# Low products at the end of each weight unit, chunk outputs written by ScalarE's queue, shifted reads spaced, last norm on VectorE alone

## The chip, the core and the metric

The kernel runs on one core of one Trainium2 chip. The metric is the device time of one execution in microseconds (us); a change within 0.5% of it counts as no change. Six parts are changed together in this case, most of them in the first quarter of the program.

## What is computed

One layer of a hybrid decoder for 320 columns of tokens (256 of a prompt, and 8 samples of 8). A normalised input h goes through one combined projection into three mixers side by side, and a SwiGLU block follows:

```
h = rmsnorm(x);  proj = h @ w_in             # 2048 -> a_val, a_gate, b_u, b_v, c_u
A: z = a_val * sigmoid(a_gate); 31-tap causal depthwise conv of z; layer norm per head; silu
B: chunks of 128 positions: u * (tril(w_s) @ layernorm(v) + b_s)
C: per group of 16 channels a complex diagonal state of 64 (h_t = a h_{t-1} + B u_t),
   y = Re(C h) + d u;  z = gelu(y);  gl = z @ w_glu;  out = gl_1 * sigmoid(gl_2)
x += concat(A, B, C) @ w_out;   x += (silu(h2 @ w_gate) * (h2 @ w_up)) @ w_down
y = rmsnorm(x)                               # and the new states
```

## The kernel before

**Units.** The large weights come from DRAM in units of eight 128x128 tiles (512 KB, tile `raw`, SyncE's queue, L201). ScalarE rounds a unit to `hi` (L208), VectorE takes the rest, `lo = raw - hi` (L215, recorded at L52). TensorE makes three products of each tile: `hi` by the high part of the input (L237), `hi` by its low part (L238), `lo` by the high part (L240); 24 products for a unit. There are three buffers each of `raw` and `hi`, two of `lo`. Three accumulators in PSUM are called `acc`, two `sm`, three `sc`. Unit u's loop body (L1297 on) loads unit u + 3, splits `hi` of u + 2 and `lo` of u + 1, and then issues its products in four quarters.

**The order of units.** ORDER (L26) lists the projection: C tiles (inputs of the state mixer), K0 to K3 (the convolution of a head, 32 small products of 128x32 weights and more, L577), A and U tiles, and V (L1018 to L1022, the `v` rows in products of 512 columns). The loop over all other weights follows from about 320 us on.

**Side work.** Everything else (recurrence, preparation of states, norms, gates) is written as generators that yield. After each quarter of a unit `Side.run` (L122) steps those with priority under 1, and then VectorE's work (priority 1 and over) as long as VectorE's modelled time `vec.t` is not past TensorE's modelled time `pe`. So this rule alone sets where VectorE's recurrence operations stand among the `lo` splits, and through waits such as `until` also where TensorE's products of the mixers stand among the units.

**Convolution reads.** `conv_in` (L541 on) writes a head's row to DRAM (`zr`), and reads it back in four shifted copies `z4` by GpSimd's queue (L556); `row_load` brings the next head's row.

**State mixer's output.** A group of 128 channels i (0 to 7, called y0 to y7 here) is computed by products with the states H (L914 to L916). ScalarE applies the gelu and gives `z` (L922). `z_layout` (L927 on) writes z to DRAM (`dz`, SyncE's queue), waits, and reads it back in another layout as `zc` (four reads); the GLU products read zc (L949, L950).

**Tail.** After the last unit the norm's row `r` is made, and 16 tiles of the output are multiplied by it and written out (L1366 to L1370).

Of the kernel before, what the change touches and what calls it, by code (L numbers as in the profile page):

```python
# [15 lines left out]
NT = 320  # L16
# [4 lines left out]
MULT, ADD, SUB = ALU.mult, ALU.add, ALU.subtract  # L21
# [10 lines left out]
def build(nc, tc, I, O):  # L32
    with ExitStack() as ctx:
        ctx.enter_context(tc.manual_schedule())
        _build(ctx, nc, tc, I, O)
# [65 lines left out]
class Side:  # L101
# [22 lines left out]
    def run(self):  # L124

        self.now += 1
        for t in list(self.live):
            if t.prio < 1 and t.due <= self.now and not t.done:
                self.step(t)
        skip = None  # L130
        while self.vec.t <= self.pe:
            ready = [t for t in self.live if t.due <= self.now and t.prio >= 1]
            if not ready:
                break
            t = ready[0]
            if t is skip:
                if len(ready) > 1 and ready[1].prio < GAP:
                    t = ready[1]
                else:
                    self.vec.t += 0.13  # L140
            skip = t if self.step(t) == "gap" else None
        self.vec.t = max(self.vec.t, self.pe - 0.5)
# [12 lines left out]
def _build(ctx, nc, tc, I, O):  # L155
    A, G, T = nc.scalar, nc.gpsimd, nc.tensor
    V = Vec(nc.vector)
    side = Side(V)
# [11 lines left out]
    def acc():  # L170
        return pacc.tile([128, 512], F32, tag="acc", name="acc")
# [4 lines left out]
    def sc():  # L176
        return psc.tile([128, 512], F32, tag="sc", name="sc")
# [4 lines left out]
    def tmp(tag, shape=(128, NT), dt=F32, bufs=1):  # L182
        return mp.tile(list(shape), dt, tag=tag, name=tag, bufs=bufs)
# [4 lines left out]
    S = {}  # L188
# [28 lines left out]
    class Box:  # L217
        ps = None

    def tile_units(src, rows, post, need=None, psum=acc):  # L220

        n = src.shape[1] // 128
        box = Box()

        def make(u, m):
            def pre():
                if need is not None:
                    need()
                if u == 0:
                    box.ps = psum()  # L230

            def mm(hi, lo, a, b):
                r = rows()
                ps = box.ps[:, :NT]
                for j in range(a, b):
                    c = slice(j * 128, j * 128 + 128)
                    T.matmul(ps, hi[:, c], r[u + j][0], start=u + j == 0, stop=False)  # L237
                    T.matmul(ps, hi[:, c], r[u + j][1], start=False, stop=False)  # L238
                for j in range(a, b):
                    T.matmul(ps, lo[:, j * 128:j * 128 + 128], r[u + j][0], start=False, stop=u + j == n - 1)  # L240
            return pre, mm

        out = []
        for u in range(0, n, 8):
            m = min(8, n - u)
            pre, mm = make(u, m)
            out.append((src[:, u * 128:(u + m) * 128], m * 128, mm, m * 0.44, pre,
                        (lambda: post(box.ps[:, :NT])) if u + m == n else None))
        return out
# [71 lines left out]
    E = Later(V)  # L321
# [206 lines left out]
    def post_val(h):  # L528
        def f(ps):
            row, gs, r = S["row", h], S["gs", h], S["rstd"]  # L530
            V.scalar_tensor_tensor(gs, gs, 1.0, ps, op0=ADD, op1=MULT)
            V.scalar_tensor_tensor(row[:, 30:286], gs[:, 0:NP], 0.5, r[:, 0:NP], op0=MULT, op1=MULT)
            V.scalar_tensor_tensor(samples(row)[:, :, 30:38], gs[:, NP:].rearrange("p (s t) -> p s t", s=8), 0.5,
                                   r[:, NP:].rearrange("p (s t) -> p s t", s=8), op0=MULT, op1=MULT)
            side.add(0.3, conv_in(h))
        return f

    def row_load(h):

        S["row", h] = tmp("row", (128, ZW), bufs=2)  # L540
        G.dma_start(S["row", h], I["rows"][h])  # L541

    def conv_in(h):

        row = zrows[h]
        yield Wait(2)
        G.dma_start(row, S["row", h])
        yield Wait(5)
        if h < 2:
            row_load(h + 2)  # L550
        while h and ("k", h - 1) not in S:
            yield Wait(1)
        z4 = S["z4", h] = tmp("z4", (128, 4, Z4))
        base = row[0:1, 0:1]
        for g in range(4):
            G.dma_start(z4[:, g], bass.AP(tensor=base.tensor, offset=base.offset + 32 * g * ZW,  # L556
                                           ap=[[1, 4], [ZW, 32], [1, Z4]]))

    def k_pre(h):
        def f():  # L560
            side.until(lambda: ("z4", h) in S)
            S["kps", h] = acc()
        return f

    def k_mm(h):
# [337 lines left out]
    def c_out():  # L903

        H, U = S["H"], S["U"]
        side.add(0.3, c_glu())
        for i in range(8):
            while side.now < S.get(("mat due", i), 1e9) or i - S["glu"] >= 3 or ("rec", i // 4) not in S:
                yield Wait(1)
            bd, Tt = S["mats"].pop(i)  # L910
            py = sc()
            for p in range(4):
                o = py[:, 80 * p:80 * p + 80]
                T.matmul(o, cat(bd[:, 0, p, 1:5]), H[:, 0, 4 * i + p, 0:80], start=True, stop=False)  # L914
                T.matmul(o, cat(bd[:, 1, p, 1:5]), H[:, 1, 4 * i + p, 0:80], start=False, stop=False)  # L915
                T.matmul(o, Tt[:, p, :], U[:, i, p, :], start=False, stop=True)  # L916
            side.pe += 1.65
            S["y"] = i + 1
            z = tmp("z", (128, 4, 80))
            py = py[:, :NT].rearrange("p (a q) -> p a q", a=4)  # L920
            for c in (slice(0, 64), slice(64, 80)):
                A.activation(z[:, :, c].rearrange("p a (b r) -> p a r b", b=8),  # L922
                             py[:, :, c].rearrange("p a (r b) -> p a r b", b=8), AF.Gelu_apprx_tanh)
            side.add(0.2, z_layout(i, z))
            yield Wait(2)

    def z_layout(i, z):  # L927
        zc = S["zc", i] = tmp("zc", (128, 4, 80), bufs=3)
        dz = dp.tile([128, 4, 80], F32, tag="dz", name="dz")
        yield Wait(2)  # L930
        nc.sync.dma_start(dz, z)
        yield Wait(4)
        for p in range(4):
            nc.sync.dma_start(zc[32 * p:32 * p + 32], dz[:, p, :].rearrange("(j g) q -> g j q", j=4))
        S["z due", i] = side.now + 3

    def c_glu():
        crows, half = [], {}
# [232 lines left out]
    def rstd2(neg=False):  # L1171
        if "rstd" not in Q:
            g = inv_sqrt(Q["fp"], Q["pv"][:, :NT], [128, NT], "rs2", neg, 16.0)
            while "rstd" not in Q:
                try:
                    next(g)
                except StopIteration as e:
                    Q["rstd"] = e.value
        return Q["rstd"]
# [64 lines left out]
    for t in ORDER:  # L1244
        if t[0] == "A":
            a_tiles(int(t[1]))
        elif t[0] == "K":
            h = int(t[1])
# [48 lines left out]
    for u, d in enumerate(units):  # L1297
# [31 lines left out]
        if u in (100, 102, 104, 106):  # L1329
            h = (u - 100) // 2  # L1330
# [13 lines left out]
        n = d["n"] // 128  # L1344
# [16 lines left out]
    r = rstd2(True)  # L1361

    def rows(q, a, b):
        return X["xa"][q][:, a:b, :]

    for E, q, a, b in ((G, 3, 0, 2), (G, 3, 2, 4), (V, 0, 0, 1), (V, 0, 1, 4), (V, 1, 0, 4), (V, 2, 0, 3), (V, 2, 3, 4)):  # L1366
        E.tensor_tensor(rows(q, a, b), rows(q, a, b), r[:, None, :].to_broadcast([128, b - a, NT]), op=MULT)
    for E, q, a, b in ((nc.sync, 0, 0, 1), (nc.scalar, 0, 1, 4), (nc.sync, 3, 0, 2), (nc.scalar, 1, 0, 4),
                       (nc.sync, 3, 2, 4), (nc.scalar, 2, 0, 3), (nc.sync, 2, 3, 4)):
        E.dma_start(O["yT"][:, 4 * q + a:4 * q + b, :], rows(q, a, b))  # L1370

_OUT = {
    "yT": (128, 16, 320), "rows": (4, 128, ZW), "nss": (128, 2, 32, 9), "ncv": (64, 512),
# [86 lines left out]
```

## Time and profile before

| what | value |
|---|---|
| median of 3 runs | 1352.18 us (1348.64 to 1353.87) |
| the profiled execution | 1352.68 us, span 1351.0 us |
| mean granted TensorE clock | 0.989 of full speed |
| TensorE busy | 1318.4 us, 98% of the span |
| VectorE busy | 721.8 us, 53% |
| ScalarE busy | 565.8 us, 42% |

The span is the time from the first to the last recorded instruction; the time of the execution is 1.7 us longer. PE is TensorE, DVE is VectorE, ACT is ScalarE, POOL is GpSimd, SP is SyncE; a q behind a name is the engine's own instruction queue. The granted clock is a share of 2.4 GHz; 0.5 is the lower of its two levels, 1.2 GHz.

### The profile page before, as it was taken

The numbers are of one execution on the slowest core, as the hardware profiler recorded it, in microseconds if no ns is written. First come the engines' busy times: TensorE is split into PE (matmuls) and PEld (weight loads), VectorE is DVE, ScalarE is ACT, GpSimd is POOL, SyncE is SP. The second block draws the span as 40 slices with busy tenths as digits, with TensorE's granted clock in tenths as the row PEclk, the third lists the DMA queues.
The fourth block names the chain that finished last, engine by engine and source line by source line (L and its number), as shares of the span: only waits on it lengthen the run. The fifth ranks groups of instructions, "written<-read, shape, count | busy, mean of one in ns | idle before, by whom it ended". The sixth has DMA issues, their size and how long they took to land.

```text
span 1351.0 us, 22667 instructions
## 1 busy us (share of the span) xinstructions
PE 1318.4 (98%) x9324; PEld 1290.4 (96%) x9324; DVE 721.8 (53%) x1195; ACT 565.8 (42%) x824; POOL 71.9 (5%) x101
## 2 busy tenths in 40 slices
PE   8999999999999999999999999999999999999995
PEld 8888987899999999999999999999999999999995
DVE  8867986685555444444444444444444444434444
ACT  7378535474454333333333333333233333322452
POOL 1110101010130000000000000000000000000112
PEclk9999998999999999999999999999999999999998
DMA  7784576564444554444444444555444445554453
GB/s 261 194 204 133 142 187 161 168 210 141 149 147 142 175 173 148 148 141 157 155 146 151 141 157 155 147 150 152 146 156 145 152 141 158 155 148 141 142 152 121
DMA packets 78584, 212.49 MB, mean 157 GB/s; under 512 B 20640, under 2 KB 28064, under 8 KB 78416
## 3 DMA queue, kind: packets, MB, share of 16 engines
q1 hardware_dynamic: 71440, 198.34, 46.6%
q0 software_dynamic: 6176, 10.94, 3.2%
q8 instruction: 73, 1.20, 0.4%
q10 hardware_dynamic: 864, 1.76, 0.3%
q14 instruction: 31, 0.25, 0.1%
HBM read 203.47 MB, written 8.73 MB: 157 GB/s over the span
## 4 chain that ended last, share of the span: by engine, by line
PE 90%; DVE 4%; DMA 3%; ACT 2%; issue 1%; SPq 0%; DVEq 0%; ACTq 0%
PE acc L240 28%; PE acc L237 28%; PE acc L238 28%; DMA raw<-in_win 2%; DVE lo L52 1%; PE acc L577 1%; PE sc L758 1%; PE sc L914 1%; PE acc L1018 1%; PE sc L915 1%; PE sc L916 1%; PE acc L1020 1%; PE acc L1019 1%; PE sc L770 0%; ACT hi L208 0%
## 5 line engine op out<-in xcount | busy, mean ns | idle before, releaser
L52 DVE TENSOR_TENSOR lo<-raw,hi 128x1024 fp32r<-128x1024 f32 (+1 forms) x357 | 421.3, 1181 | 213.5 <-issue 164.0
L208 ACT ACTIVATE hi<-raw 128x1024 fp32r<-128x1024 f32 (+2 forms) x361 | 369.3, 1024 | 340.1 <-PE acc L238 246.5
L237 PE MATMUL acc<-hh,hi 128*128 128x320 f32 x1408 | 424.4, 309 | 0.0
L238 PE MATMUL acc<-hl,hi 128*128 128x320 f32 x1408 | 422.8, 308 | 0.0
L240 PE MATMUL acc<-hh,lo 128*128 128x320 f32 x1408 | 321.0, 308 | 0.0
L237 PEld LDWEIGHTS acc<-hh,hi 128*128 128x128 f32 x1408 | 264.4, 188 | 0.1
L238 PEld LDWEIGHTS acc<-hl,hi 128*128 128x128 f32 x1408 | 264.4, 188 | 0.1
L240 PEld LDWEIGHTS acc<-hh,lo 128*128 128x128 f32 x1408 | 234.7, 188 | 0.0
L237 PE MATMUL acc<-fh,hi 128*128 128x320 f32 x704 | 212.0, 309 | 0.0
L238 PE MATMUL acc<-fl,hi 128*128 128x320 f32 x704 | 211.8, 308 | 0.0
L240 PE MATMUL acc<-fh,lo 128*128 128x320 f32 x704 | 165.5, 308 | 0.0
L237 PEld LDWEIGHTS acc<-fh,hi 128*128 128x128 f32 x704 | 132.2, 188 | 0.0
L238 PEld LDWEIGHTS acc<-fl,hi 128*128 128x128 f32 x704 | 132.1, 188 | 0.0
L240 PEld LDWEIGHTS acc<-fh,lo 128*128 128x128 f32 x704 | 118.9, 188 | 0.0
L52 DVE TENSOR_TENSOR xa<-acc,xa 128x320 f32<-128x320 f32 x80 | 39.3, 491 | 127.8 <-PE acc L240 127.8
L237 PE MATMUL acc<-xh,hi 128*128 128x320 f32 x288 | 91.2, 324 | 2.0 <-ACT hi L208 2.0
L1210 ACT ACTIVATE fh<-fu 128x320 fp32r<-128x320 f32 x44 | 20.8, 472 | 163.0 <-DVE fu L52 163.0
L238 PE MATMUL acc<-xl,hi 128*128 128x320 f32 x288 | 87.8, 312 | 0.0
L1188 ACT ACTIVATE fg<-fg 128x320 f32<-128x320 f32 x44 | 20.8, 472 | 138.9 <-DVE fg L52 138.9
L52 DVE TENSOR_TENSOR fu<-acc,rs 128x320 f32<-128x320 f32 x44 | 21.6, 492 | 98.0 <-PE acc L240 98.0
L52 DVE TENSOR_TENSOR fg<-acc,rs 128x320 f32<-128x320 f32 x44 | 21.6, 492 | 95.9 <-PE acc L240 95.9
L240 PE MATMUL acc<-xh,lo 128*128 128x320 f32 x288 | 66.9, 314 | 4.4 <-DVE lo L52 4.4
(255 smaller groups left out, 1353.5 us busy)
## 6 DMA issues: line engine op xcount, KB each, us to landing
raw<-in_wgu SPq DMA_DIRECT2D x176, 512.0 KB, 3.5
raw<-in_wdn SPq DMA_DIRECT2D x80, 512.0 KB, 3.6
raw<-in_win SPq DMA_DIRECT2D x37, 512.0 KB, 4.5
raw<-in_wout SPq DMA_DIRECT2D x32, 512.0 KB, 3.5
z<-zr POOLq DMA_DIRECT2D x16, 296.0 KB, 12.6
raw<-in_wv SPq DMA_DIRECT2D x8, 512.0 KB, 4.2
raw<-in_wdn SPq DMA_DIRECT2D x16, 256.0 KB, 2.6
xa<-in_xT SPq DMA_DIRECT2D x4, 640.0 KB, 7.5
```

What stands on the lines that cost most here:

```text
L52: return self.v.tensor_tensor(out, a, b, op=op)
L208: A.activation(d["hi"][:, o], d["raw"][:, o], AF.Copy)
L237: T.matmul(ps, hi[:, c], r[u + j][0], start=u + j == 0, stop=False)
L238: T.matmul(ps, hi[:, c], r[u + j][1], start=False, stop=False)
L240: T.matmul(ps, lo[:, j * 128:j * 128 + 128], r[u + j][0], start=False, stop=u + j == n - 1)
L577: T.matmul(ps[c, o:o + n], w[:, 32 * (8 * g + j):32 * (8 * g + j) + 32], x, start=j == 0, stop=j == 7, tile_position=(0, 32 * g))
L758: T.matmul(pe[:, 80 * p:80 * p + 80], ps[ri][:, p, :], U[:, ct, p, :], start=True, stop=True)
L914: T.matmul(o, cat(bd[:, 0, p, 1:5]), H[:, 0, 4 * i + p, 0:80], start=True, stop=False)
L915: T.matmul(o, cat(bd[:, 1, p, 1:5]), H[:, 1, 4 * i + p, 0:80], start=False, stop=False)
L916: T.matmul(o, Tt[:, p, :], U[:, i, p, :], start=False, stop=True)
L1188: A.activation(gs, gs, AF.Silu)
L1210: A.activation(h, ub, AF.Copy)
```

## The change

1. The planner lets VectorE's modelled time run up to 2.0 us ahead of TensorE's.
2. In a unit all 16 `hi` products stand first, the 8 `lo` products behind them (before: per pair of tiles 4 `hi`, then 2 `lo`).
3. `conv_in` waits two planner steps before each of the four shifted reads.
4. Head 3's convolution takes its accumulator from `sc` in place of `acc`.
5. `dz` is written by ScalarE's queue without a wait ahead of it; the reads of `zc` follow five steps later, and what depends on them is due a step later.
6. The last norm's 16 tiles are multiplied by VectorE in six operations (before: five on VectorE, two on GpSimd), and written by six transfers in place of seven.

```
-        while self.vec.t <= self.pe:
+        while self.vec.t <= self.pe + 2.0:
...
-                for j in range(a, b):
-                    c = slice(j * 128, j * 128 + 128)
-                    T.matmul(ps, hi[:, c], r[u + j][0], start=u + j == 0, stop=False)
-                    T.matmul(ps, hi[:, c], r[u + j][1], start=False, stop=False)
-                for j in range(a, b):
-                    T.matmul(ps, lo[:, j * 128:j * 128 + 128], r[u + j][0], start=False, stop=u + j == n - 1)
+                todo = [(hi, j, i) for j in range(m) for i in range(2)] + [(lo, j, 0) for j in range(m)]
+                for w, j, i in todo[3 * a:3 * b]:
+                    T.matmul(ps, w[:, j * 128:j * 128 + 128], r[u + j][i], start=w is hi and u + j + i == 0,
+                             stop=w is lo and u + j == n - 1)
...
         for g in range(4):
+            yield Wait(2)
             G.dma_start(z4[:, g], bass.AP(tensor=base.tensor, offset=base.offset + 32 * g * ZW,
...
-            S["kps", h] = acc()
+            S["kps", h] = sc() if h == 3 else acc()
...
-        yield Wait(2)
-        nc.sync.dma_start(dz, z)
-        yield Wait(4)
+        nc.scalar.dma_start(dz, z)
+        yield Wait(5)
...
-        S["z due", i] = side.now + 3
+        S["z due", i] = side.now + 4
...
-    for E, q, a, b in ((G, 3, 0, 2), (G, 3, 2, 4), (V, 0, 0, 1), (V, 0, 1, 4), (V, 1, 0, 4), (V, 2, 0, 3), (V, 2, 3, 4)):
-        E.tensor_tensor(rows(q, a, b), rows(q, a, b), r[:, None, :].to_broadcast([128, b - a, NT]), op=MULT)
+    for n, (q, a, b) in enumerate(((0, 0, 1), (0, 1, 4), (1, 0, 4), (2, 0, 4), (3, 0, 3), (3, 3, 4))):
+        V.tensor_tensor(rows(q, a, b), rows(q, a, b), r[:, None, :].to_broadcast([128, b - a, NT]), op=MULT)
+        (nc.scalar if n % 2 else nc.sync).dma_start(O["yT"][:, 4 * q + a:4 * q + b, :], rows(q, a, b))
```

How TensorE's order changes at y0, the first output of the state mixer. Before, y0 (L914 to L916, the name H is the state) follows the last `lo` products of a finished unit:

```order
L237 MATMUL acc<-xh,hi 128x320
L238 MATMUL acc<-xl,hi 128x320
L237 MATMUL acc<-xh,hi 128x320
L238 MATMUL acc<-xl,hi 128x320
L240 MATMUL acc<-xh,lo 128x320 x2
L914 MATMUL sc<-H,m 128x80
L915 MATMUL sc<-H,m 128x80
L916 MATMUL sc<-U,m 128x80
```

Now (line numbers are smaller by one to three) it stands behind the first quarter of a unit, and 18 products of that unit are still to come behind it:

```order
L237 MATMUL acc<-xh,lo 128x320 x8
L237 MATMUL acc<-xh,hi 128x320
L237 MATMUL acc<-xl,hi 128x320
L237 MATMUL acc<-xh,hi 128x320
L237 MATMUL acc<-xl,hi 128x320
L237 MATMUL acc<-xh,hi 128x320
L237 MATMUL acc<-xl,hi 128x320
L913 MATMUL sc<-H,m 128x80
L914 MATMUL sc<-H,m 128x80
L915 MATMUL sc<-U,m 128x80
```

The same piece shows the new order of a unit: its eight `lo` products stand in one row at its end, and y0 is 18 products earlier than before.

On GpSimd, the four shifted reads of heads 0 and 1 (z_707 and z_1027) with their neighbours before:

```order
L547 DMA zr<-row 128x596 x2
L541 DMA row<-in_rows 128x596
L556 DMA z_707<-zr 128x1x592 x4
L541 DMA row<-in_rows 128x596
L739 MEMSET H 128x64
L556 DMA z_1027<-zr 128x1x592 x4
```

and now:

```order
L545 DMA zr<-row 128x596 x2
L539 DMA row<-in_rows 128x596 x2
L555 DMA z_707<-zr 128x1x592 x4
L738 MEMSET H 128x64
L555 DMA z_1027<-zr 128x1x592 x4
```

Head 0's reads have a second row load ahead of them, and the four reads of a head still follow one another with nothing between them. For heads 2 and 3 one or two other transfers (the parameters `craw`, the weights `wg`) now stand among the four.

## Rows read from the trace of the kernel before

**Rows 1.** The profile page: busy time, share and instructions of each engine.

```profile
PE 1318.4 (98%) x9324; PEld 1290.4 (96%) x9324; DVE 721.8 (53%) x1195; ACT 565.8 (42%) x824; POOL 71.9 (5%) x101
```

**Rows 2.** Windows: span, then busy us of PE, PEld, DVE, ACT, POOL; clock, DMA.

```profile
65.00:71.00 6.00, 4.74 (x20) 4.48 (x21) 4.51 (x14) 2.00 (x3) 0.00 (x0) 0.73 0.72 216
180.00:200.00 20.00, 17.60 (x155) 15.22 (x153) 17.67 (x44) 7.60 (x10) 0.59 (x1) 1.00 0.57 193
200.00:214.00 14.00, 11.49 (x134) 9.17 (x133) 10.65 (x36) 6.25 (x15) 3.49 (x5) 1.00 0.72 150
214.00:225.00 11.00, 11.00 (x53) 9.36 (x52) 2.47 (x11) 4.39 (x13) 0.59 (x1) 0.53 0.55 147
225.00:256.00 31.00, 30.31 (x180) 23.69 (x182) 25.56 (x61) 18.16 (x44) 2.17 (x4) 1.00 0.55 170
256.00:320.00 64.00, 63.10 (x517) 58.89 (x510) 44.54 (x80) 42.72 (x67) 5.85 (x14) 1.00 0.56 182
320.00:1330.00 1010.00, 1010.00 (x6890) 1009.84 (x6889) 467.61 (x560) 368.60 (x449) 29.65 (x29) 1.00 0.47 150
```

**Rows 3.** What PE waited for: us in total, times, longest.

```profile
PE acc L240 <- DVE lo L52: 4.4, 5, 1.6
PE sc L770 <- ACT H L759: 2.9, 2, 1.5
PE acc L237 <- ACT hi L208: 2.0, 2, 1.2
PE sc L949 <- issue: 1.9, 1, 1.9
```

**Rows 4.** Timeline of PE: start, duration, instruction, idle before it and its releaser.

```profile
7.86 0.41 PE L238 MATMUL sc<-xl,hi 128*128 128x320 f32 x1 [1.34 <-DVE xl L56]
...
34.52 0.56 PE L240 MATMUL acc<-xh,lo 128*128 128x320 f32 x2 [1.56 <-DVE lo L52]
...
50.93 0.56 PE L240 MATMUL acc<-xh,lo 128*128 128x320 f32 x2 [0.86 <-DVE lo L52]
...
65.85 0.41 PE L237 MATMUL acc<-xh,hi 128*128 128x320 f32 x1 [1.16 <-ACT hi L208]
...
75.29 1.07 PE L577 MATMUL acc<-z,hi 128*32 128x256 f32 x16
...
191.91 0.42 PE L914 MATMUL sc<-H,m 128*128 128x80 f32 x2
...
213.44 0.78 PE L949 MATMUL sc<-zc,wg 128*128 128x320 f32 x2 [1.88 <-issue]
...
251.56 0.41 PE L914 MATMUL sc<-H,wv 128*128 128x80 f32 x2
```

**Rows 5.** Timeline of ACT: a split, and a load of function tables.

```profile
68.41 1.06 ACT L208 ACTIVATE hi<-raw 128x1024 fp32r<-128x1024 f32 x1 [2.61 <-DMA raw<-in_win]
...
100.40 1.28 ACT L611 ACT_TABLE_LOAD   x1
```

**Rows 6.** The page's DMA issues: count, KB of each, median us to landing.

```profile
z<-zr POOLq DMA_DIRECT2D x16, 296.0 KB, 12.6
...
zr<-row POOLq DMA_DIRECT2D x4, 298.0 KB, 3.4
```

**Rows 7.** Timeline of DVE: the last operations of the recurrence's two parts.

```profile
191.35 0.42 DVE L52 TENSOR_TENSOR H<-lnv 128x256 f32<-128x256 f32 x1
...
251.03 0.42 DVE L52 TENSOR_TENSOR H<-lnv 128x256 f32<-128x256 f32 x1
```

**Rows 8.** What SyncE's queue waited for: us in total, times, longest.

```profile
SPq L931 <- ACT z L922: 23.4, 8, 4.4
```

**Rows 9.** Timeline of the tail: VectorE's and GpSimd's multiplications.

```profile
1339.40 7.10 DVE L52 TENSOR_TENSOR xa<-xa,rs 128x320 f32<-128x320 f32 x5
1339.44 4.24 POOL L1367 TENSOR_TENSOR xa<-xa,rs 128x640 f32<-128x640 f32 x2 [7.29 <-DVE rs L56]
```

**Rows 10.** Tile xa in the tail: duration ns min/median/max of VectorE's five operations.

```profile
L52 DVE TENSOR_TENSOR xa<-xa,rs x5: 479/1145/2814, 1339.4 to 1346.0; 128x320 f32<-128x320 f32 x2, 128x960 f32<-128x960 f32 x2, 128x1280 f32<-128x1280 f32 x1
```

**Rows 11.** Groups by shape: VectorE on four tiles at once, busy us, mean ns.

```profile
L52 DVE TENSOR_TENSOR H<-H,U 128x1280 f32<-128x1280 f32 x1 | 1.5, 1486 | 0.0
```

More of the change, by code (lines that the diff above doesn't have):

```diff
@@ L1364, in rows @@
         return X["xa"][q][:, a:b, :]
-    for E, q, a, b in ((G, 3, 0, 2), (G, 3, 2, 4), (V, 0, 0, 1), (V, 0, 1, 4), (V, 1, 0, 4), (V, 2, 0, 3), (V, 2, 3, 4)):
-        E.tensor_tensor(rows(q, a, b), rows(q, a, b), r[:, None, :].to_broadcast([128, b - a, NT]), op=MULT)
-    for E, q, a, b in ((nc.sync, 0, 0, 1), (nc.scalar, 0, 1, 4), (nc.sync, 3, 0, 2), (nc.scalar, 1, 0, 4),
-                       (nc.sync, 3, 2, 4), (nc.scalar, 2, 0, 3), (nc.sync, 2, 3, 4)):
-        E.dma_start(O["yT"][:, 4 * q + a:4 * q + b, :], rows(q, a, b))
+    for n, (q, a, b) in enumerate(((0, 0, 1), (0, 1, 4), (1, 0, 4), (2, 0, 4), (3, 0, 3), (3, 3, 4))):
+        V.tensor_tensor(rows(q, a, b), rows(q, a, b), r[:, None, :].to_broadcast([128, b - a, NT]), op=MULT)
+        (nc.scalar if n % 2 else nc.sync).dma_start(O["yT"][:, 4 * q + a:4 * q + b, :], rows(q, a, b))
 _OUT = {
```

## The prediction

> **What bounds the kernel now.** I read the page's busy shares first: TensorE works in 98% of the span [rows 1], so the question is only where the other 2%, and time at a low clock, lie. The table of windows answers it [rows 2]. From 320 to 1330 us TensorE is busy in all of 1010.00 us, at full clock, 6890 products, so 1010.00 / 6890 = 0.1466 us for a product. Three quarters of the program can't be helped by any part of this change; they could only be harmed. Before 320 us and in the tail TensorE idles: 1351.0 - 1318.4 = 32.6 us in all [rows 1]. To this come stretches that count as busy but ran at a low clock: 0.53 from 214 to 225 us, 0.73 from 65 to 71 us [rows 2]. Third, the list of waits says whom TensorE waits for [rows 3]: VectorE's `lo` 4.4 us, ScalarE's copies of H 2.9, `hi` 2.0, one issue at the first GLU 1.9. The timeline places them [rows 4]. The sum goes by the profiled execution, 1352.68 us, which is 0.5 us above the median of the runs.
>
> **Start, to 13 us.** TensorE waits 1.34 us at 7.86 us for the input's low part [rows 4]. In the new order a unit's third pair of `hi` products stands two `lo` products earlier than before, so it wants the input split earlier, and the `lo` wait shrinks. I take +0.5 us; below it nothing is lost, above it four to eight products (8 x 0.1466 = 1.2).
>
> **To 80 us.** A unit's first `lo` product moves from the fifth place to the 17th, 12 x 0.1466 = 1.76 us later. The longest wait for `lo` is 1.6 [rows 3], so these waits should go: 1.56 and 0.86 here, 2.4 us [rows 4]. `hi` of a unit is also free 8 products (1.2 us) earlier, which is to help the wait of 1.16 us at 65.85. Then the unit after it becomes late: its `hi` starts at 68.41 when the raw load lands and takes 1.06, so is ready at 69.47 [rows 5]. Its products began at 75.29 - 24 x 0.1466 = 71.77 [rows 4], so 2.3 us can be had if that load lands no sooner. Against this stands K0, which needs the shifted reads. On GpSimd a second row load now stands ahead of them and its buffer is free only when the second `zr` write has landed, 3.4 us by the median [rows 6], and they go out that much later at the worst, while each lands 12.6 us later [rows 6]. I take -2, between -3.5 (2.3 and the 1.2 of the earlier `hi`) and +1 (K0 waits for its late reads).
>
> **80 to 180 us.** The two waits for copies of H, 2.9 us [rows 3], are not touched by `lo`. ScalarE now loads a function table (1.28 us [rows 5]) ahead of those copies rather than behind, and the planner's lead of 2.0 us puts more VectorE work ahead. Head 1's reads are adjacent as before, so the spacing does nothing there. I take 0, from -2 to +3.
>
> **180 to 192 us.** TensorE idles 20.00 - 17.60 = 2.4 us to 200 us [rows 2]: waits for `hi` and `lo`. These can go. But y0 needs the recurrence's first part, whose last operation ended at 191.35 + 0.42 = 191.77 [rows 7], 0.14 us before y0 started [rows 4]: here VectorE is the bound. The order moves four operations of 0.42 us of it ahead of `lo` splits, so it ends some 1.7 us earlier, and y0 is asked for 18 x 0.1466 = 2.6 us earlier in the row of products. TensorE waits there for the difference, 0.9, and loses it; in exchange the waits ahead of y0 stop mattering. I take -0.5, from -2.5 to +1.2.
>
> **192 to 225 us.** The largest term. Idle time is 14.00 - 11.49 = 2.5 us from 200 to 214 [rows 2], of it 1.88 at the first GLU product at 213.44 [rows 4], which needs zc of y0. The same stretch then shows the granted clock at 0.53 for 11.0 us, near the lower level (1.2 GHz), after TensorE had stood still at 213.44. At full clock the work would take 11.0 x 0.53 = 5.8 us, so 5.2 us are at stake. SyncE's queue stood 23.4 us in eight waits for the gelu, 4.4 at most [rows 8], with raw loads and zc reads behind them. Now ScalarE writes dz itself right behind its gelu, and with y0 1.7 us earlier zc is ready before the GLU. Both the stall and the drop should go: -2.5 - 5.2 = -7.7; I take -7, from -7.7 to 0. A rule speaks against this part. The Trainium skill (DMA: Bandwidth & Descriptors, "Issuing engines are not separate DMA queues") says that starting transfers from several engines saves only the sequencer's time of issuing, since all run on the same 16 DMA engines. By the rule the stall of 1.88 would stay, and with it the drop; what the row counts is another thing than issuing, a queue that waits for its data.
>
> **225 to 256 us.** Idle 31.00 - 30.31 = 0.69 [rows 2]. y4 at 251.56 starts 0.11 us after the recurrence's second part ends at 251.45 [rows 4, 7]. It is now asked for eight of V's products earlier, by the order. The mean product of this stretch takes 30.31 / 180 = 0.17 us [rows 2], V's 512 columns more than that by the ratio of 512 to 320 at most (0.1466 x 1.6 = 0.235); eight are 1.4 to 1.9 us, which TensorE may wait. I take +1, from -1 to +3.
>
> **256 to 320 us.** Idle 64.00 - 63.10 = 0.9 [rows 2]. ScalarE has two more table loads there, 2 x 1.28 = 2.6 us [rows 5], but works 42.72 of 64 us, so it can hide them; head 3's accumulator frees an `acc` and takes an `sc`. I take 0, from -0.9 (the idle time) to +4 (both loads and a wait for `sc`). The Trainium skill (ScalarE: Activation LUTs, "What ACT_TABLE_LOAD costs") counts about 2.66 us for a change of table, a drain included. By it the two would be 5.3 us of ScalarE rather than 2.6, still hidden, and the upper end 6.7; the row shows 1.28 for the load itself.
>
> **320 to 1330 us.** Nothing: no wait is there to remove, and `lo` is only asked for later.
>
> **Tail.** VectorE took 7.10 us for 12 of the 16 tiles while GpSimd worked beside it for 4.24 [rows 9]. Its four-tile operation took 2.81 us beside GpSimd [rows 10], while an operation of that shape takes 1.49 elsewhere [rows 11]; three tiles took 1.15 alone, one 0.48 [rows 10]. Six operations: 0.48 + 1.15 + 1.49 + 1.49 + 1.15 + 0.48 = 6.2, so -0.9 against 7.10. From -1.3 (the smaller last transfer too) to -0.3 (the transfers out become the bound).
>
> **Sum.** +0.5 - 2 + 0 - 0.5 - 7 + 1 + 0 - 0.9 = -8.9. 1352.68 - 8.9 = 1343.8, and 1343.3 from the median: 1343.5 us.
>
> **Rivals.** *The stall at the first GLU stays* (chance 0.24). The reads of heads 2 and 3 have only one or two transfers among them, so their 12.6 us of landing [rows 6] still fall on raw loads and on zc; something is late near 213 us as before, and the clock drops after it. Against it: dz leaves earlier. Then 7 us of the sum are lost but for about 1: 1343.5 + 6 = 1349.5. The rule of the skill on issuing engines gives this case.
>
> *Slower: TensorE runs into the recurrence* (0.11). Place: y0 and y4. Both start today within 0.14 us of VectorE's end [rows 4, 7], and both are asked for earlier (2.6 and up to 1.9 us). If the recurrence doesn't move, TensorE waits 4.5 us, and if after each wait the clock drops as it did behind 213.44, 2 x 5.2 more: 14.9, less the 2, 2.5 and 0.9 of other terms, +9.5: 1362. It decides when VectorE ends more than about 1.5 us after TensorE arrives. Against it: the planner puts recurrence operations ahead of `lo`.
>
> *A larger gain* (0.10). Nearly all waits of rows 3 go and the low clock at 65 to 71 us (6 x 0.27 = 1.6 us) too, and y0 and y4 come without a wait (1 each): -8.9 - 2.9 - 1.6 - 2 = -15.4, so 1337.
>
> **How the numbers follow.** My forecast has 0.55, with its own range of 1338 to 1348. A measurement of this kernel can't tell less than 0.5% (6.8 us) from no change, so faster means below 1345.4. Of my 0.55, 0.44 lie below it and 0.11 above; the first rival gives 0.22 to no change and 0.02 to slower; the second 0.11 to slower, the third 0.10 to faster. Faster 0.54, no change 0.33, slower 0.13. The range goes from 1335, some 2 us under the third rival, to 1354: it leaves out the second rival and the tails of the others.
>
> **What would show it.** Waits of TensorE for `lo` in the list near zero; the first GLU product with no idle time ahead of it and a granted clock of 1.00 behind it; y0 with an idle time of about a microsecond released by VectorE; K0 about 2 us earlier; VectorE's last group of multiplications at 6.2 us. If the stretch from 320 to 1330 us is not 1010 us, or if clock drops show up at new places before 320 us, I was wrong in kind.

## The result and the profile after

The changed kernel is slower: 1357.86 us (median of 7 executions, 1354.43 to 1360.78) against 1349.61 us (7 executions, 1345.90 to 1353.87), a ratio of 1.0057 with a 95% interval of 1.0036 to 1.0079. I had forecast 1343.5 us and at most 1354, from three runs of before with a median of 1352.18; as a ratio that is 0.9936. By the half per cent that counts as no change this is just a change, and the interval reaches below it. The profiled execution took 1355.53 us with a span of 1353.8, one of the shorter ones; that of before (1352.68) was one of the longer. The two profiles differ by 2.9 us where the medians differ by 8.3, so a step is judged below by the profiles of many kernels, not by this pair alone.

The windows of the changed kernel, with the columns of [rows 2]; two stretches are new, 84 to 93 and 192 to 202 us:

```profile
65.00:71.00 6.00, 5.65 (x38) 5.38 (x38) 4.42 (x17) 1.06 (x1) 0.00 (x0) 1.00 0.85 208
84.00:93.00 9.00, 6.87 (x24) 5.92 (x25) 4.94 (x13) 7.76 (x16) 0.00 (x0) 0.63 1.15 172
180.00:200.00 20.00, 16.57 (x94) 16.07 (x94) 15.45 (x40) 7.49 (x12) 0.58 (x1) 0.80 0.63 187
192.00:202.00 10.00, 9.22 (x40) 9.26 (x41) 8.18 (x23) 3.67 (x6) 0.04 (x1) 0.51 0.42 146
214.00:225.00 11.00, 11.00 (x73) 9.09 (x72) 9.08 (x33) 6.72 (x18) 3.08 (x6) 1.00 0.87 172
225.00:256.00 31.00, 29.17 (x161) 22.85 (x161) 25.19 (x62) 17.57 (x43) 1.78 (x4) 1.00 0.69 202
256.00:320.00 64.00, 60.80 (x504) 55.63 (x503) 42.68 (x79) 45.57 (x71) 8.87 (x14) 1.00 0.52 173
320.00:1330.00 1010.00, 1010.00 (x6894) 1009.84 (x6893) 469.20 (x562) 362.72 (x448) 28.72 (x29) 1.00 0.47 151
```

From 320 to 1330 us nothing moved: 6894 products in 1010 us against 6890. From 214 to 225 us the clock is now 1.00, as forecast. The low clock stands elsewhere: 0.63 from 84 to 93 us and 0.51 from 192 to 202 us. From 225 to 320 us TensorE idles 5.0 us, before 1.6 [rows 2].

What TensorE waited for, as in [rows 3]:

```profile
PE sm L597 <- ACT of L585: 3.7, 1, 3.7
PE sc L237 <- DVE xl L56: 2.9, 3, 1.8
PE sc L913 <- DVE H L52: 2.7, 1, 2.7
PE sc L769 <- ACT H L758: 2.3, 3, 1.5
PE sm L605 <- ACT of L602: 2.2, 2, 1.1
PE sc L947 <- issue: 2.1, 1, 2.1
```

The 4.4 us of waits for `lo` are nearly gone, as they should be. In their place stand single, longer waits (in the order of the list: for the copy of K0's result, for the input's low part, for the state H ahead of y0). The timeline of TensorE places them (columns as in [rows 4]):

```profile
8.70 0.64 PE L237 MATMUL sc<-xl,hi 128*128 128x320 f32 x1 [1.77 <-DVE xl L56]
...
73.07 4.55 PE L576 MATMUL acc<-z,hi 128*32 128x256 f32 x128 [0.57 <-ACT hi L208]
...
85.03 0.81 PE L597 MATMUL sm<-of,cent 128*128 128x320 f32 x2 [3.71 <-ACT of L585]
...
192.78 0.69 PE L913 MATMUL sc<-H,m 128*128 128x80 f32 x2 [2.71 <-DVE H L52]
...
282.69 0.78 PE L947 MATMUL sc<-zc,wg 128*128 128x320 f32 x2 [2.11 <-issue]
```

K0 starts at 73.07 in place of 75.29. That is the size of the 2 us I had counted, and 12 us later 3.71 are given back: ScalarE's copy of K0's result (`of`, L585) comes late. At y0 TensorE waits 2.71 us for VectorE.

The tail, as in [rows 9] and [rows 10]:

```profile
1343.34 5.83 DVE L52 TENSOR_TENSOR xa<-xa,rs 128x320 f32<-128x320 f32 x6
```

Six operations alone take 5.83 us, seven on two engines took 7.10. From the start of these multiplications to the end of the span it is 1353.8 - 1343.34 = 10.5 us, before 1351.0 - 1339.40 = 11.6.

### The profile page after: what moved, and what is told of

Its sections match the earlier page's. It is cut to its first block, busy times and chain, and to the rows that moved or that the text cites. A ratio compares the mean times of both kernels' runs of the same rounds, so it can differ in the third digit from the quotient of the medians.

```text
span 1353.8 us, 22658 instructions
## 1 busy us (share of the span) xinstructions
PE 1317.6 (97%) x9324; PEld 1290.0 (95%) x9324; DVE 720.9 (53%) x1196; ACT 563.8 (42%) x826; POOL 70.5 (5%) x99
## 4 chain that ended last, share of the span: by engine, by line
PE 86%; DVE 5%; DMA 4%; ACT 3%; issue 1%; SPq 0%; DVEq 0%; ACTq 0%
PE acc L237 80%; DMA raw<-in_win 4%; DVE lo L52 1%; ACT hi L208 1%; DVE lnv L52 1%; PE sc L913 1%; PE sc L914 1%; PE sc L915 1%; DVE H L52 1%; PE sc L757 1%; DVE xa L52 0%; ACT bd L695 0%; DVE g L52 0%; ACT m L695 0%; PE sc L576 0%
## 5 line engine op out<-in xcount | busy, mean ns | idle before, releaser
L208 ACT ACTIVATE hi<-raw 128x1024 fp32r<-128x1024 f32 (+2 forms) x361 | 364.4, 1024 | 270.5 <-PE acc L237 184.2
L237 PE MATMUL acc<-hh,hi 128*128 128x320 f32 x1408 | 416.0, 309 | 0.0
L237 PE MATMUL acc<-hl,hi 128*128 128x320 f32 x1408 | 415.6, 308 | 0.0
L237 PE MATMUL acc<-hh,lo 128*128 128x320 f32 x1408 | 235.1, 308 | 0.0
L237 PEld LDWEIGHTS acc<-hh,lo 128*128 128x128 f32 x1408 | 213.6, 188 | 0.0
L237 PE MATMUL acc<-fh,hi 128*128 128x320 f32 x704 | 207.4, 309 | 0.0
L237 PE MATMUL acc<-fl,hi 128*128 128x320 f32 x704 | 207.2, 308 | 0.0
L237 PE MATMUL acc<-fh,lo 128*128 128x320 f32 x704 | 118.3, 308 | 0.0
L237 PEld LDWEIGHTS acc<-fh,lo 128*128 128x128 f32 x704 | 106.7, 188 | 0.0
L237 PEld LDWEIGHTS acc<-xh,hi 128*128 128x128 f32 x288 | 56.0, 194 | 3.3 <-ACT hi L208 1.6
```

Source lines behind the costliest of these rows:

```text
L208: A.activation(d["hi"][:, o], d["raw"][:, o], AF.Copy)
L237: T.matmul(ps, w[:, j * 128:j * 128 + 128], r[u + j][i], start=w is hi and u + j + i == 0, stop=w is lo and u + j == n - 1)
```

## The experiments

All ratios are to the kernel before, from 5 rounds (12 executions of a kernel, 7 of one), with a 95% interval. An experiment's times and those of before spread over some 5 to 17 us, so a difference between two ratios is uncertain by about 0.0025; smaller differences are given by their medians and show only a direction.

**First, one part undone at a time.** The theories: A, the lead asks for y0 before VectorE has the states; B, the transfers are at fault; C, ScalarE's queue is.

```
no_lead:     -  while self.vec.t <= self.pe + 2.0:     +  while self.vec.t <= self.pe:
no_lo_last:  old order of products in tile_units
no_spacing:  -  yield Wait(2)   (ahead of each shifted read)
no_act_dz:   -  nc.scalar.dma_start(dz, z); Wait(5)    +  Wait(2); nc.sync.dma_start(dz, z); Wait(4), z due as before
```

> The changed kernel with the planner's lead of 2.0 us taken back; the other five parts stay. Theory A (the lead asks for y0 and y4 before VectorE has the states): y0 stands 18 products later again, TensorE's wait of 2.7 us for the state H ahead of y0 and the low clock behind it (about 4 us) go, y4's 1.9 us too; the time falls by about 8 us from 1357.9 to about 1349.5, ratio to before 1.000 or less. Theory B (the transfers are at fault: head 1's shifted reads fall on raw loads, so ScalarE evicts head 0's result late, 3.7 us at 85 us, and the clock falls after it): that stall stays and the time stays at 1355 to 1358, ratio 1.005. Theory C (ScalarE's queue is blocked by its dz writes): stays at 1.005 too.

> The changed kernel with the old order of products in a unit (pairs of tiles, low products between). Theory A: y0 and y4 stand as in the changed kernel, the wait at y0 stays and the waits for lo come back (about 4 us): 1360 or more, ratio 1.007 to 1.010. Theory B: without the early arrival of TensorE at head 0's convolution the reads of head 1 go out later and the stall at 85 us shrinks from 3.7 us to under 1: 1353 to 1355, ratio 1.003. A third reading, that the new order itself is harmful at the start (input split wanted earlier, 2.9 us of waits for the input's low part against 1.7): 1.2 us less than 1357.9.

> The changed kernel without the four waits of two planner steps ahead of the shifted reads. Theory B: head 0's and head 1's reads are adjacent either way, but head 0's go out ahead of the second row load again, up to 4 us earlier; raw loads behind them land differently, and the stall at 85 us changes by over 1 us: ratio 1.000 to 1.003. Theories A and C: no change from the changed kernel, 1.0057 within 0.002.

> The changed kernel with dz written by SyncE's queue again, and the old waits. Theory C: ScalarE is free of eight transfers that wait for earlier ones, the waits of TensorE for ScalarE behind 230 us (2.1 us at 283, 1.3 at 243, 1.1 at 298) go: about 4 us less, 1354, ratio 1.002. Theory A: the first GLU is late again by about 2 us, or nothing changes: 1.006 to 1.008. Theory B: no change, 1.0057.

| undone | median us | ratio | interval |
|---|---|---|---|
| lead | 1353.47 | 1.0021 | 1.0004 to 1.0039 |
| low products last | 1355.17 | 1.0036 | 1.0018 to 1.0053 |
| spacing | 1355.67 | 1.0030 | 1.0010 to 1.0049 |
| ScalarE's dz | 1357.39 | 1.0063 | 1.0037 to 1.0088 |

No single part carries the loss. By the medians each of three parts undone gives some back, none all of it (0.0036, 0.0021 and 0.0027; only the first is clearly above the uncertainty). Taking ScalarE's dz back gives nothing, so theory C falls. Theory A wanted 1.000 for the first row and 1.007 or more for the second, and missed both; theory B met its range in the third row, came near in the second (1.003) and missed in the first (1.005). And without the lead y0 still waited 1.80 us for H, though it stood 18 products later again.

**Second, single parts on the kernel before, and pairs.**

```
spacing_alone:  before, with  + yield Wait(2)  ahead of each shifted read
lead_alone:     before, with  + 2.0  in the planner's condition
neither:        the changed kernel, without both
lo_and_tail:    before, with low products last and the new tail
```

> The kernel before with the four planner waits ahead of the shifted reads as the only edit. Theory A (each of lead and spacing costs by itself): head 0's reads go out behind the second row load, some 2.5 us later; the reads of U behind them on SyncE's queue start about 1.5 us later, ScalarE evicts head 0's result about 3 us later (84 in place of 81.4 us), and TensorE waits there: 1352 to 1355, ratio 1.002 to 1.004. Rival (the spacing costs only where TensorE comes early through the other parts): no change, ratio 1.000 within 0.002.

> The kernel before with the planner's lead of 2.0 us as the only edit. Theory A: y0 stands 18 products earlier, TensorE waits for VectorE's states there (some 2 to 3 us) and the clock drops behind it; y4 and the fifth GLU wait 2 to 3 us: 1354 to 1357, ratio 1.003 to 1.005. Rival: the lead only hurts where the low products stand last, since then TensorE comes early: ratio 1.000 within 0.002.

> The changed kernel without the lead and without the spacing; low products last, the sc accumulator, ScalarE's dz and the tail stay. Theory A: both harmful parts are gone; the tail gives 1.2 us and the low products 1 to 3: 1346 to 1349, ratio 0.997 to 0.9985. Rival (the rest is harmful too, TensorE's early arrival is only given back at the next wait for ScalarE): ratio 1.000 to 1.002.

> The kernel before with the low products last and the new tail as the only edits. Theory A: 1.2 us from the tail, 1 to 2 us from the waits for lo: ratio 0.997 to 0.999, the same as without lead and spacing, so that dz and the accumulator do nothing. Rival (ScalarE's dz is what helps at the first GLU): slower than that kernel by about 2 us, ratio 0.9995 to 1.001.

| kernel | median us | ratio | interval |
|---|---|---|---|
| spacing alone | 1354.52 | 1.0022 | 1.0005 to 1.0039 |
| lead alone | 1350.69 | 1.0003 | 0.9987 to 1.0019 |
| without lead and spacing | 1351.29 | 1.0009 | 0.9989 to 1.0030 |
| low products last and tail | 1354.23 | 1.0033 | 1.0011 to 1.0055 |

The last row was the surprise, outside both expectations. The part from which I had expected the gain at K0 costs by itself, although the tail in the same kernel takes 5.83 us in place of 7.10. Without lead and spacing nothing is gained either; theory A's 0.997 to 0.9985 was a miss. The spacing met theory A; the lead alone did not (1.003 to 1.005 was expected).

**Third, the low products by themselves (theory D) and what is left without them (theory E).**

```
lo_alone:        before, with low products last
dz_and_tail:     before, with ScalarE's dz, head 3's accumulator, the new tail
lo_after_start:  neither, with  + if S["unit"] < 2: (old order)
lead_dz_tail:    dz_and_tail, with  + 2.0  in the planner's condition
```

> The kernel before with the low products last in a unit as the only edit. Theory D (the waits for lo only change their name: the raw load behind them is late, so TensorE waits for hi instead, and at y0 for VectorE's state H, and the input's low part is wanted earlier at the start): nothing is gained by 65 us, y0 shows a wait of about 1.8 us for H, ratio 1.002 to 1.005. Rival (the low products are harmless and the slow time of the kernel with low products and tail came by chance or from the tail): ratio 0.999 to 1.001.

> The kernel before with ScalarE's dz, head 3's accumulator and the new tail; no lead, no spacing, old order of products. Theory E (dz takes away the stall at the first GLU, the tail 1.2 us): no idle time ahead of the first GLU, ratio 0.997 to 0.9985. Rival (the stall comes back at another GLU, as ScalarE's other work is late): ratio 0.999 to 1.001.

> As the kernel without lead and without spacing, but the first two units keep the old order of products. If the start is what the low products cost (1 us of waits for the input's low part, and what follows from VectorE's later row): 1 to 2 us less than 1.0009, ratio 0.998 to 1.000. If the cost is at y0 (theory D's later half): no change, 1.0009 within 0.001.

> As the kernel with ScalarE's dz, the accumulator and the tail, with the planner's lead of 2.0 us too. If the lead costs only where the low products stand last (alone it made 1.0003): within 0.001 of that kernel, ratio 0.997 to 0.999, and y0 comes with no wait for H. If the lead costs by itself: 0.003 above it, ratio 1.000 to 1.002.

| kernel | median us | ratio | interval |
|---|---|---|---|
| low products last alone | 1354.53 | 1.0023 | 1.0002 to 1.0045 |
| dz, accumulator, tail | 1347.73 | 0.9975 | 0.9962 to 0.9988 |
| without lead and spacing, old order in two units | 1351.94 | 1.0008 | 0.9994 to 1.0022 |
| dz, accumulator, tail and lead | 1351.84 | 1.0004 | 0.9989 to 1.0019 |

Theory D holds in sign, theory E fully: dz, accumulator and tail alone beat both kernels. That the start is where the low products cost is not shown (1.0008 as with 1.0009, which a cost of 2 or 3 us could still hide). The lead costs 0.0029 on this base, with the low products between their tiles, so it does not need them to be harmful; on the kernel before, without ScalarE's dz, it cost nothing (1.0003).

**Fourth, where and by what.** The base is the kernel of 0.9975.

```
lo_to_k1:          base, low products last where S["unit"] <= 24
lo_around_y0:      base, low products last where 24 < S["unit"] < 38
lo_after_y0:       base, low products last where S["unit"] >= 38
spaced_row_later:  base, with Wait(2) ahead of each read and row_load(h + 2) behind the four reads
sc_and_tail:       base, with dz by SyncE and its old waits
dz_and_tail_again: base
```

> The kernel with ScalarE's dz, the accumulator and the new tail (0.9975), with the low products last only in the units ahead of head 1's convolution (to about 130 us). If their cost lies there (the wait for lo only becomes one for hi, and larger single waits let the clock fall): ratio 1.000 to 1.001, as with low products last everywhere (1.0009). If it lies at y0 (theory D's later half): 0.9975 within 0.001.

> The same base with the low products last only in the units behind y0 (from about 190 us to the end). If the cost lies before or at y0: 0.9975 within 0.001. If it lies behind (VectorE's and ScalarE's later waits at 223 and 286 us): 1.000 or more.

> The same base with the four planner waits ahead of the shifted reads, but the next row's load issued behind the reads. If the spacing costs through the second row load that stands ahead of head 0's reads: head 0's reads go out at about 51.5 us and the ratio stays at 0.9975 within 0.001. If it costs through the waits themselves (other heads' reads and what the planner puts in their place): 0.9995 to 1.001.

> The same base with dz written by SyncE's queue again: only head 3's accumulator and the new tail are left of the change. If dz is what gains at the first GLU: the stall of 1 to 2 us there is back and the ratio is 0.9985 to 1.000. If accumulator and tail give the gain: 0.9975 within 0.001.

> The same base (ScalarE's dz, accumulator, new tail) with the low products last only in the units between head 1's convolution and y0. If the larger part of their cost lies here (TensorE comes to y0 before VectorE has the states, waits 1 to 2 us there and the clock falls): ratio 0.999 to 1.001. If it is spread over the program evenly: 0.998 to 0.999. If there is none here: 0.9975.

> The base itself once more (ScalarE's dz, accumulator, new tail; no lead, no spacing, old order of products). If its gain is no accident of the executions: ratio 0.9965 to 0.9985 again; if it is: 0.999 to 1.000, the tail alone.

| kernel | median us | ratio | interval |
|---|---|---|---|
| low last to 130 us | 1347.81 | 0.9985 | 0.9970 to 0.9999 |
| low last around y0 | 1351.43 | 0.9995 | 0.9980 to 1.0010 |
| low last behind y0 | 1349.26 | 0.9989 | 0.9972 to 1.0005 |
| spaced, row load behind | 1350.58 | 1.0001 | 0.9985 to 1.0016 |
| accumulator and tail | 1349.73 | 0.9996 | 0.9976 to 1.0016 |
| base again | 1348.71 | 0.9974 | 0.9954 to 0.9993 |

By the medians the low products cost most around y0 (0.0020 above the base); the other two pieces cost 0.0010 and 0.0014. Each of the three is within the uncertainty, so the times alone do not place the cost. The granted clock, which every execution gives, does so better: its mean over 12 executions is 0.9931 and 0.9927 for the base, 0.9902 with the low products last around y0, and 0.9919 in each of the other two. Estimated from this, 0.0027 of some 1318 us of busy TensorE are 3.6 us; the medians of the base and of the kernel with low products last around y0, taken in one set, differ by 2.7 us.

The gain of the base stands. With the row load behind the reads the spacing still costs 0.0026, so the row load is not the whole of it. By the medians dz by ScalarE gives 0.0021 of the base's 0.0025, tail and accumulator the rest; that division is within the uncertainty, and on the changed kernel taking dz back cost only 0.0006.

## Why the prediction was wrong, point by point

By ratios that build on one another: base 0.9975; with the low products 1.0009 (about +4.6 us of 1350); with the lead as well 1.0030 (+2.8); with the spacing 1.0057 (+3.6). The order matters: the lead's step here is within the uncertainty, while taking the lead out of the changed kernel gave 0.0036. The gains I had named are in the first number, 3.4 us. The losses come from three parts that I had priced at zero or as gains.

**180 to 192 us, -0.5: the step that failed.** I let the recurrence end 1.7 us earlier because four of its operations stand ahead of `lo` splits, and TensorE wait 0.9 us for it. This is VectorE in the changed kernel (columns as in [rows 7]):

```profile
184.17 0.25 DVE L56 SCALAR_TENSOR_TENSOR kpad<-id,dsk,sc 128x32 f32<-128x32 f32 x1 [5.00 <-ACT kpad L884]
...
191.08 1.22 DVE L52 TENSOR_TENSOR lo<-raw,hi 128x1024 fp32r<-128x1024 f32 x1
192.21 0.42 DVE L52 TENSOR_TENSOR H<-lnv 128x256 f32<-128x256 f32 x1
```

The last operation ends at 192.63, 0.86 us later than before (191.77), and TensorE waits 2.71 us. The order of a queue says nothing of when its head may go. `kpad`, for which VectorE stands 5.00 us, comes on ScalarE right behind a `hi` split (L208) that waits for its raw load. This is that split before and in the changed kernel:

```profile
181.38 1.06 ACT L208 ACTIVATE hi<-raw 128x1024 fp32r<-128x1024 f32 x1 [3.65 <-DMA raw<-in_win]
```

```profile
182.94 1.06 ACT L208 ACTIVATE hi<-raw 128x1024 fp32r<-128x1024 f32 x1 [4.39 <-DMA raw<-in_win]
```

From the start of this split to y0 it is 10.53 us before and 9.84 in the changed kernel, and nearly the same in the others: 10.53 to 10.55 in eleven profiles without the lead, 9.83 or 9.84 in five with it (10.26 to 11.06 in the other four), and in all twenty the split waited for its raw load. So the new order of VectorE was worth 0.7 us and not 1.7, and the raw load, which my sum did not have, came 1.56 us later. Together that is the 0.87 us by which y0 starts later than before. Why the load is later I leave open.

What TensorE had mostly waited for ahead of y0 was `lo`, which in VectorE's queue stands close to the recurrence. This is the longest such wait of this stretch before:

```profile
188.68 0.56 PE L240 MATMUL acc<-xh,lo 128*128 128x320 f32 x2 [1.15 <-DVE lo L52]
```

With the low products last that wait is gone and TensorE runs into the recurrence itself. Two kernels without the lead show it, first the base with the old order, then the low products last alone:

```profile
188.54 0.42 PE L914 MATMUL sc<-H,m 128*128 128x80 f32 x2
```

```profile
188.48 0.42 PE L912 MATMUL sc<-H,m 128*128 128x80 f32 x2 [1.34 <-DVE H L52]
```

In these two y0 starts at the same time, and in 18 of the 20 profiles, with the wait or without it, 0.14 to 0.16 us behind VectorE's last operation. The wait for H ahead of y0 (1.34 to 2.71 us) is in all nine kernels that have the low products last in the units ahead of y0, and in none of the other eleven profiles (waits of 0.5 us and more counted, one profile of each kernel, two of the base). In seven of the nine a low clock follows, in none of the eleven. The time from the start of y0 to K2 measures it, since these products are then all ready: 2.7 to 2.8 us in all eight profiles with the old order of y0 that come to it without a wait, 5.3, 5.3, 4.2 and 4.2 in four with the wait, 2.8 in two. With the lead's order it is 8.1 or 8.2 without the wait and 9.7, 11.3 and 12.6 with it. So the wait itself costs little (y0 could not start earlier), the clock behind it up to 12.6 - 8.1 = 4.5 us. That the wait brings the low clock is read from this coincidence; no run makes the one without the other on purpose. This was my second rival, in the place I gave it; I let the planner's order speak against it and gave it 0.11. y4 was not part of it: it starts 0.95 us later than before, with no wait. Below, the windows behind y0 in two kernels with the same wait, 1.79 us (columns as in [rows 2]); the first, without lead and spacing, keeps the clock at full, the second, with the low products last only around y0, falls to the lower level:

```profile
193.00:198.00 5.00, 4.94 (x64) 4.08 (x68) 4.90 (x13) 3.85 (x7) 0.00 (x0) 1.00 0.67 241
```

```profile
192.00:198.00 6.00, 5.81 (x32) 5.47 (x36) 5.87 (x16) 2.44 (x3) 0.00 (x0) 0.51 0.52 182
```

**To 80 us, -2, and 80 to 180 us, 0.** The first came out in the profile (-2.2), but by luck: in the eleven profiles with the old order of products up to K0 it starts at 72.97 to 75.29, with a mean of 73.8, in the nine with the new order at 72.07 to 75.82, with a mean of 73.4. Before was the latest of the eleven, so the new order is worth some 0.4 us there, not 2, and that is within the spread. The second was wrong by 4.6: K1 starts 2.4 us later than before (135.04 and 132.62). The step failed by taking time won at K0 as won. Behind K0 the next product needs ScalarE's `of`, which stands behind `hi` splits that wait for raw loads. ScalarE's copy in four kernels (columns as in [rows 5]): before, changed, spacing alone, and the base:

```profile
81.42 0.51 ACT L586 ACTIVATE of<-acc,cv 128x320 f32<-128x320 f32 x1
```

```profile
84.47 0.51 ACT L585 ACTIVATE of<-acc,cv 128x320 f32<-128x320 f32 x1
```

```profile
83.08 0.51 ACT L587 ACTIVATE of<-acc,cv 128x320 f32<-128x320 f32 x1
```

```profile
81.24 0.51 ACT L586 ACTIVATE of<-acc,cv 128x320 f32<-128x320 f32 x1
```

With the spacing it comes at 83.08 to 84.59 in the five kernels that have it with the row load ahead, and at 80.82 to 82.76 in the fourteen profiles without it. This is SyncE's queue in the same order before, changed, spacing alone:

```profile
68.76 2.64 SPq L647 DMA_DIRECT2D U<-du  x4
```

```profile
70.51 2.64 SPq L646 DMA_DIRECT2D U<-du  x4
```

```profile
69.57 2.65 SPq L648 DMA_DIRECT2D U<-du  x4
```

The raw loads stand behind these reads of U on SyncE's in-order queue, and the reads wait for a write (`du`). In the changed kernel that write is itself issued 1.66 us later than before (61.20 and 59.54); with the spacing alone it is not (59.62), and U still goes out 0.81 us later. Head 0's shifted reads, which take long to land [rows 6], go out at 51.41 before, 56.11 in the changed kernel, 54.36 with the spacing alone. That these late reads hold U up was my theory, and the run with the row load behind the reads speaks against it: there they go out at 50.71, and U goes out at 69.48 all the same. What makes U late is open. That TensorE comes to K0 earlier is then worth nothing: with the spacing alone

```profile
83.64 0.81 PE L599 MATMUL sm<-of,cent 128*128 128x320 f32 x2 [2.39 <-ACT of L587]
```

I had put the second row load into the upper end of the first step (+1) and nowhere else. With the row load moved behind the reads `of` comes at 82.22, between the spacing alone and the base; that kernel still lost 0.0026, in its profile with 2.81 us for a `hi` at 186 us and 2.40 at a GLU at 279 us.

**192 to 225 us, -7.** The mechanism was right and the size too large. With dz by ScalarE none of thirteen profiles has a stall at the first GLU; with SyncE's dz four of seven have one (0.84 to 3.18 us), and two more wait 1.84 and 4.00 at the fourth. The first GLU with only accumulator and tail:

```profile
215.36 0.78 PE L949 MATMUL sc<-zc,wg 128*128 128x320 f32 x2 [3.18 <-DMA zc<-dz]
```

By the medians it is worth 0.0021, 2.8 us, not 7. I counted the stall and the clock drop of one profile as if every execution had them: behind the first GLU the clock falls (0.50 to 0.55) in three of the seven profiles with SyncE's dz. And 0.63 of the 2.5 us idle that I counted stood at 207.15, for another copy (`of`).

**256 to 320 us, 0.** 3.2 us idle in place of 0.9. The sixth GLU waits 2.11 us in the changed kernel. Such a wait (1.45 to 3.32 us) stands there in all six kernels with the lead and in one of the three with the spacing but not the lead; in the others it is 1.13 at most. The list names no releaser, but GpSimd's queue has it, where the GLU's weights `wg` are loaded. Before, with the sixth GLU at 278.49, and in the changed kernel:

```profile
270.55 0.55 POOL L719 DMA_DIRECT2D wg<-in_wglu  x1
```

```profile
274.66 3.49 POOL L989 TENSOR_SCALAR_AFFINE_SELECT z<-z 128x128 f32<-128x128 f32 x4 [5.08 <-DMA z<-in_wst]
278.10 0.55 POOL L718 DMA_DIRECT2D wg<-in_wglu  x1
```

The load of 278.10 lands 4.5 us later, at 282.6, and the GLU starts at 282.69. In all nine profiles with a wait of 0.9 us or more at this GLU it starts within 0.2 us of this landing. So the load goes out late, behind masking operations that themselves wait for a load; my sum had no term for GpSimd's queue. With the lead on the base the wait is the longest stall of its profile, and the granted clock behind it is 0.71 as far as 285 us, which would account for the lead's cost there; the lead alone has 1.45 us, full clock, and no cost:

```profile
274.68 1.40 PE L948 MATMUL sc<-zc,wg 128*128 128x320 f32 x2 [3.07 <-issue]
```

SyncE's queue, in the changed kernel, now waits for dz to land rather than for the gelu, for longer than the 23.4 us of [rows 8]:

```profile
SPq L932 <- DMA dz<-z: 30.7, 6, 8.0
```

The Trainium skill's rule (DMA: Bandwidth & Descriptors, "Issuing engines are not separate DMA queues") lets another engine's queue save only the time of issuing. The trace half agrees: the wait moved from one entry of SyncE's queue to the next, but the first GLU got its data in time.

**Start, +0.5.** 10.0 us busy by 13 us became 8.3, so 1.7 us were lost and not 0.5, more than my upper end of 1.2; with the clock at 0.80 in place of 0.87. The first two units in the old order won back 0.9 us by 13 us (10.25 busy against 9.33, without lead and spacing), but TensorE then waited 1.21 us for the input's low part at 26.92, and the time did not change by what the runs can resolve.

**225 to 256 us, +1, and tail, -0.9.** 1.8 us idle, 0.7 before: the number is right, but by luck, since y4 came without the wait that I had put there. The idle time is 0.54 us for zc at the fourth GLU and this, for a copy by ScalarE:

```profile
242.59 0.66 PE L873 MATMUL sc<-m,bbd 128*32 128x128 f32 x14 [1.29 <-ACT m L695]
```

The tail, -1.1 (10.5 us and 11.6), was right in size and cause.

What stays open: by what the spacing costs, why the raw load ahead of y0 and the reads of U come later, and how the low products' 0.0044, added over three pieces, divide outside the stretch around y0.

## What to carry to other kernels

A stall's time in one profile is no price: first see whether the next wait behind it has the same source (a late load, a queue in order), since then TensorE only arrives earlier at that one. Several short waits between products can be cheaper than one long wait, because the clock may fall behind the long one (here behind waits of 1.45 to 2.71 us ahead of y0). And ask what releases an engine's queue before counting what a new order in it wins. Try each part of a change by itself: here three losing parts hid a version (dz by ScalarE's queue, head 3's accumulator, the tail on VectorE) that takes 0.9975 of the time, a gain still within the half per cent that counts as no change.

## What the runs showed of the hardware that I had not expected

The same kernel's executions differ by more than the whole change: before took 1344.05 to 1359.93 us within one set of 35. The granted clock goes with part of it: in that set the executions under 1349 us have a mean clock of 0.992 to 0.995, those over 1353 us 0.986 to 0.993. In the profiles, from 13 to 320 us the base keeps 1.00 (0.99 in its second profile), the changed kernel 0.97 and the kernel of low products and tail 0.96; estimated, the last is 288.49 x 0.04 = 11.5 us of busy time. Before has 0.97 there too, so one profile of each does not separate it from the changed kernel (columns as in [rows 2]; base, changed, low products and tail):

```profile
13.00:320.00 307.00, 290.73 (x2401) 265.44 (x2400) 240.09 (x608) 188.68 (x357) 36.08 (x52) 1.00 0.62 181
```

```profile
13.00:320.00 307.00, 288.70 (x2333) 263.07 (x2332) 235.25 (x604) 188.92 (x357) 33.46 (x52) 0.97 0.62 176
```

```profile
13.00:320.00 307.00, 288.49 (x2312) 262.03 (x2312) 233.12 (x600) 184.39 (x353) 30.86 (x52) 0.96 0.61 174
```

The same wait does not always bring the fall. At 65 us the kernel with the lead alone waits 0.99 us and keeps 1.00 to 71 us, before waited 1.16 and had 0.73 [rows 2, 4]; the base waits 1.56 and keeps 1.00.
